# Norms of a two-layer hybrid DiT block: sums of squares kept as a running sum, first weights split before the norm, two modulation units behind it

## The chip, the cores and the metric

The kernel runs on one core of a Trainium2 chip. It is written with a tile framework: the program issues operations in Python order, a list scheduler decides before the run in which order each engine takes its instructions, and every engine then works through its own list in that order. DMAs are issued by SyncE (SP), whose list is in order too. The metric is the device time of one execution in microseconds (us), lower is better. Times of unprofiled runs are given as a median; a profiled execution gives the trace.

## What is computed

A DiT of two layers on 256 context and 256 latent tokens, width 1024, all in float32. In each layer a norm with modulation feeds a mixer of three branches (gated delta net, gated linear attention, differential attention), whose merged output goes through `w_out` into the residual. A second norm with modulation feeds a dense SwiGLU (layer 0) or a mixture of 8 experts of which each token takes 2 (layer 1, latent tokens only). The change concerns the norms and the modulation:

```python
def _rmsnorm(x, g):
    y = x * lax.rsqrt(jnp.mean(jnp.square(x), axis=-1, keepdims=True) + EPS)
    return y * g
def _modulate(x, g, shift, scale):
    return _rmsnorm(x, g) * (1.0 + scale) + shift
...
# shift and scale, and the gates of the residuals, are rows of silu(cond) @ w_mod[l] + b_mod[l]
# (6 x 1024 numbers a layer, one set for context and one for latent tokens)
```

## The kernel before

**Layout.** Everything is held with features on the 128 partitions: `x[0]` and `x[1]` are the context and the latent tokens, 8 k-blocks of 128 features by 256 tokens each. A projection of 128 output features over 512 tokens sums over the 8 k-blocks.

**Matmuls in three parts.** To keep float32 precision, each weight and each activation is split into a high part (a CAST on ScalarE, ACT, in `split`, L269) and a remainder (a subtraction on VectorE, DVE, L270). Each weight tile then takes three matmuls on TensorE (PE): `wh*ah` (L274), `wh*al` (L275), `wl*ah` (L276). Raw weights land in a pool of three buffers of 1 MB (`raw`), the split ones in six tiles (`whl`), enough for three column chunks of 128.

**A norm** (`norm_stats`, L414 on, and `norm_mod`, L434 on). For each half of the tokens: four Squares of two k-blocks each on ACT (L420, 128x512), three adds on DVE (L423), a matmul with ones that sums over partitions (L425), then Ln and Exp on ACT (L410, L411) for the reciprocal root `rs`. Then for each k-block and half: x times `rs` on DVE (L456), the modulation on ACT with scale `A` and shift `B`, which writes the high part `hh` (L457), the same in full precision on DVE (L459), and the remainder `hl` (L461). The norms are named (layer, 1 or 2): (0,1) reads inputs that `norm_only` has normed, (0,2), (1,1) and (1,2) stand behind `mix_out` of layer 0, `ffn` of layer 0 and `mix_out` of layer 1. (1,2) takes the latent half only and feeds the router (L1180).

**Residuals.** `mix_out` (L1121 on) and `ffn` (L1136 on) produce one output block of 128 features after another; behind each, one DVE operation per half adds it to x (`residual`, L1081).

**Modulation units.** `mod_unit` (L340 on) loads 1 MB of `w_mod` and runs 8 matmuls of 32 columns by 256 (L350), which the trace records as 16. A layer has 24 units, in groups of four; `mod_put` (L353 on) closes a group with a copy to SBUF on ACT (L358, tile `modr`), two short matmuls (L361) and two adds (L368). The first units run at the start; the others are spread over the mixers.

**Order of a mixer.** `PLAN` (L27 to L30) is a list of words for each layer; `m1` to `m8` place modulation units, the other words the steps of the branches (`iv` inverts the delta net's chunk matrices, `sc` is its scan, `ga`, `hc`, `gc` and so on are projections). `MOD_AHEAD` (L34 to L36) says which units a mixer takes. Words of a list are only the program order; the scheduler fills PE's waits with matmuls that stand near.

Of the kernel before, what the change touches and what calls it, by code (L numbers as in the profile page):

```python
# [26 lines left out]
PLAN = ("sm ap su m1 pr m1 iv ga1 m1 ga1 m1 ga1 m1 ga1 m1 za m1 sc m8 dec qkB m1 gb1 m1 ha ma vB m1 gla qC m1 kC m2 gc1 m1 "  # L27
        "vC m1 hb dif mb hc m1 mc",
        "sm ap m1 pr ga1 m1 iv ga1 m1 sc za m1 ga1 m1 ga1 m3 gc1 m1 qkB m1 dec vB m1 ha ma gla qC m1 kC m1 vC m1 hb dif mb "
        "hc m2 mc")  # L30
# [4 lines left out]
MOD_AHEAD = ([(0, list(range(u, u + 4))) for u in range(8, 24, 4)] + [(1, list(range(u, u + 4))) for u in range(0, 8, 4)],  # L35
             [(1, list(range(u, u + 4))) for u in range(8, 24, 4)])  # L36
# [162 lines left out]
class Prog:  # L199
# [66 lines left out]

    def split(self, hi, lo, src, n_src=None):

        self.nc.scalar.copy(hi, src)  # L269
        self.nc.vector.tensor_sub(lo, src, hi.bitcast(F32))  # L270
# [8 lines left out]
    def setup(self):  # L279
# [23 lines left out]
        self.pre = {}  # L303
        self.mod = [self.con([128, 48, 2], f"mod{l}") for l in range(2)]
# [78 lines left out]

    def mod_a(self, l, i, k0=0, k1=8):
# [29 lines left out]
    def norm_stats(self, x):  # L414
        nc = self.nc
        p = self.pq()
        sqs = []
        for k in range(0, 8, 2):
            sq = self.sd([2, 256], "sq")
            nc.scalar.activation(sq, x[:, k:k + 2], AF.Square)  # L420
            sqs.append(sq)
            if k:
                nc.vector.tensor_add(sqs[0], sqs[0], sq)  # L423
        for a in range(2):
            nc.tensor.matmul(p[:, :256], self.ones, sqs[0][:, a], start=a == 0, stop=a == 1)  # L425
        return self.rstd(p[:, :256], 256, 1.0 / DM)

    def norm_only(self, xs):

        r = self.norm_stats(xs)  # L430
# [3 lines left out]
    def norm_mod(self, l, i, x, c0, normed=False):  # L434
# [13 lines left out]
        rs = [None if normed else self.norm_stats(xs) for _, _, xs in halves]  # L448
        for k in range(8):
            for (a, m, xs), r in zip(halves, rs):  # L450
                v = slice(a - c0, a - c0 + 256)
                if normed:
                    t = xs[:, k]
                else:
                    t = self.sm([512], "nt")
# [9 lines left out]
    def proj(self, l, u, H, c0=0, c1=512):  # L465

        hh, hl = H
        w = self.pre.pop((l, u), None) or self.load(self.I["win"][l, u], [8, 256])
        for c in range(2):
            wh, wl = self.part(w[:, :, c * 128:(c + 1) * 128])  # L470
# [53 lines left out]
    def small_proj(self, l, H):  # L524
# [3 lines left out]
        wh, wl = self.part(self.load(self.I["wsm"][l], [8, 48]))  # L528
# [592 lines left out]
    def mix_out(self, l, m, x):  # L1121
        c0 = 256 * l
        n = 512 - c0
        mh, ml = self.wide(l, "mh", F32R), self.wide(l, "ml", F32R)
        for k in range(8):
            self.split(mh[k], ml[k], m[k])
        for pr in range(4):
            w = self.load(self.I["wout"][l, pr], [8, 256])
            for c in range(2):
# [4 lines left out]
                self.residual(x, 2 * pr + c, p[:, :n], c0, self.mod[l][:, 16:24])  # L1134

    def ffn(self, x, H):  # L1136
        nc = self.nc
        hh, hl = H
        for half in range(2):
            mh = [self.ch([4, 512], "fh", F32R) for _ in range(3)]  # L1140
            ml = [self.ch([4, 512], "fl", F32R) for _ in range(3)]
            for u in range(11):
                w = self.load(self.I["f13"][half * 11 + u], [8, 256])
                ps = []
                for c in range(2):
                    wh, wl = self.part(w[:, :, c * 128:(c + 1) * 128])
# [8 lines left out]
            for n in range(8):  # L1155
# [6 lines left out]
                self.residual(x, n, p, 0, self.mod[0][:, 40:48])  # L1162

# [117 lines left out]
    def experts(self, base, x):  # L1281
# [118 lines left out]
        for e in range(8):  # L1400
            for fb in range(11):
# [7 lines left out]
                if e == 0 and MOE_AT <= fb < MOE_AT + MOE_PART:  # L1409
                    self.places.append(self.ch([2, 1024], "wp", F32R))  # L1410
                if fb == 2 and e:
# [28 lines left out]
    def mixer(self, l, H):  # L1440
# [5 lines left out]
        for w in PLAN[l].split():  # L1446
            if w == "su":
                self.setup2()
            elif w == "sm":
                self.small_proj(l, H)  # L1450
            elif w == "ap":
# [36 lines left out]
    def run(self):  # L1488
# [4 lines left out]
        for i, _ in enumerate(todo):  # L1493
            if i == 0:
                x = self.load_x()
            if i in PRE:
                u = U_KA + len(self.pre)
                self.pre[0, u] = self.load(self.I["win"][0, u], [8, 256])
# [4 lines left out]
        self.mod_a(0, 1, 6, 8)  # L1503
        for l in range(2):
            H = self.norm_mod(l, 1, x, 0, l == 0)
# [14 lines left out]
            self.mix_out(l, m, x)  # L1520
# [4 lines left out]
            if l == 0:  # L1525
                H = self.norm_mod(l, 2, x, 0)
                self.ffn(x, H)
                for j in range(2):
                    self.dump(f"xf{j}", x[j])
                self.exp_tables()  # L1530
                if self.stop == "l0":
                    break
            else:
                H = self.norm_mod(l, 2, x, 256)
# [4 lines left out]
    def final(self, x):  # L1539
        nc = self.nc  # L1540
        self.exp_tables()
        rs = self.norm_stats(x)
# [30 lines left out]
```

## Time and profile before

| | |
|---|---|
| median of 3 runs | 2596.59 us (2590.91 to 2604.6) |
| profiled execution | 2588.37 us |
| its span, first to last instruction | 2586.3 us |
| mean granted TensorE clock | 0.973 of full speed |
| PE busy | 2444.9 us (95%) |
| DVE busy | 1716.4 us (66%) |
| ACT busy | 1416.6 us (55%) |

Busy times are sums over an engine's instructions. PE is busy nearly all the time, so a microsecond counts where PE waits, or where it runs at half its clock.

### The profile page before, as it was taken

The numbers are of one execution on the slowest core, as the hardware profiler recorded it, in microseconds if no ns is written. First come the engines' busy times: TensorE is split into PE (matmuls) and PEld (weight loads), VectorE is DVE, ScalarE is ACT, GpSimd is POOL, SyncE is SP. The second block draws the span as 40 slices with busy tenths as digits, with TensorE's granted clock in tenths as the row PEclk, the third lists the DMA queues.
The fourth block names the chain that finished last, engine by engine and source line by source line (L and its number), as shares of the span: only waits on it lengthen the run. The fifth ranks groups of instructions, "written<-read, shape, count | busy, mean of one in ns | idle before, by whom it ended". The sixth has DMA issues, their size and how long they took to land.

```text
span 2586.3 us, 35865 instructions
## 1 busy us (share of the span) xinstructions
PE 2444.9 (95%) x13712; PEld 1965.9 (76%) x13712; DVE 1716.4 (66%) x3130; ACT 1416.6 (55%) x2352; POOL 88.2 (3%) x216
## 2 busy tenths in 40 slices
PE   6998999999998999998978999998999999999997
PEld 4786776676676888886867878797878878878876
DVE  5585447756545434336684475767989888988987
ACT  4764343235553332335853433666877777777775
POOL 0000001100120000000000010010000000000000
PEclk8999899999998999999988999998999999999999
DMA  6344332122131223222362232257979899899994
GB/s 266 129 160 157 107 139 99 49 74 74 67 137 66 100 82 120 93 79 85 112 225 77 68 113 81 104 188 288 377 273 355 341 342 356 344 350 353 341 367 182
DMA packets 72707, 473.13 MB, mean 183 GB/s; under 512 B 8208, under 2 KB 10384, under 8 KB 19664
## 3 DMA queue, kind: packets, MB, share of 16 engines
q1 hardware_dynamic: 68208, 464.73, 48.3%
q10 hardware_dynamic: 4320, 6.03, 0.6%
q8 instruction: 110, 1.80, 0.3%
q14 instruction: 69, 0.57, 0.1%
HBM read 463.65 MB, written 7.08 MB: 182 GB/s over the span
## 4 chain that ended last, share of the span: by engine, by line
PE 70%; DVE 6%; ACT 3%; DMA 2%; issue 1%; POOL 0%; ACTq 0%; DVEq 0%; POOLq 0%
PE pm L275 16%; PE pm L274 16%; PE pm L276 16%; PE y L276 3%; PE y L275 3%; PE y L274 3%; PE la L985 1%; DMA raw<-in_win_dram 1%; PE pq L1052 1%; DVE whl L270 1%; PE pm L350 1%; PE tp L1352 1%; PE ob L996 1%; PE ob L998 1%; DVE zq L973 1%
## 5 line engine op out<-in xcount | busy, mean ns | idle before, releaser
L270 DVE TENSOR_TENSOR whl<-raw,whl 128x512 fp32r<-128x512 f32 (+2 forms) x490 | 330.7, 681 | 330.0 <-ACT whl L269 326.7
L274 PE MATMUL pm<-hh,whl 128*128 128x512 f32 (+2 forms) x1264 | 475.6, 378 | 21.3 <-ACT whl L269 7.8
L269 ACT CAST whl<-raw 128x512 fp32r<-128x512 f32 (+2 forms) x490 | 289.6, 600 | 357.1 <-PE pm L276 273.5
L276 PE MATMUL pm<-hh,whl 128*128 128x512 f32 (+2 forms) x1264 | 467.7, 371 | 7.4 <-DVE whl L270 7.4
L275 PE MATMUL pm<-hl,whl 128*128 128x512 f32 (+2 forms) x1264 | 468.3, 371 | 0.0
L270 DVE TENSOR_TENSOR wp<-rawc,wp 128x1024 fp32r<-128x1024 f32 x261 | 313.7, 1222 | 36.6 <-ACT wp L269 30.5
L274 PEld LDWEIGHTS pm<-hh,whl 128*128 128x128 f32 (+1 forms) x1264 | 243.0, 192 | 70.8 <-ACT whl L269 9.2
L269 ACT CAST wp<-rawc 128x1024 fp32r<-128x1024 f32 x261 | 268.1, 1051 | 21.0 <-PE y L276 11.4
L276 PEld LDWEIGHTS pm<-hh,whl 128*128 128x128 f32 (+1 forms) x1264 | 242.3, 192 | 48.9 <-DVE whl L270 8.4
L275 PEld LDWEIGHTS pm<-hl,whl 128*128 128x128 f32 (+1 forms) x1264 | 243.0, 192 | 43.2 <-issue 7.1
L270 DVE TENSOR_TENSOR wlo<-raw,whi 128x1024 fp32r<-128x1024 f32 x176 | 210.0, 1222 | 34.1 <-ACT whi L269 31.7
L275 PE MATMUL pm<-wlo,hg 128*128 128x512 f32 x530 | 212.1, 400 | 1.6 <-DVE wlo L270 1.4
L274 PE MATMUL pm<-whi,hg 128*128 128x512 f32 x530 | 211.2, 399 | 0.0
L276 PE MATMUL pm<-whi,hg 128*128 128x512 f32 x530 | 208.0, 392 | 0.0
L269 ACT CAST whi<-raw 128x1024 fp32r<-128x1024 f32 x176 | 178.9, 1052 | 13.2 <-PE pm L275 11.9
L275 PE MATMUL y<-wp,mt 128*128 128x512 f32 x348 | 135.4, 389 | 0.0
L276 PE MATMUL y<-wp,mt 128*128 128x512 f32 x348 | 135.3, 389 | 0.0
L275 PEld LDWEIGHTS pm<-wlo,hg 128*128 128x128 f32 x530 | 99.8, 188 | 34.6 <-DVE wlo L270 15.8
L274 PE MATMUL y<-wp,mt 128*128 128x512 f32 x348 | 120.1, 389 | 0.2 <-ACT mt L1354 0.2
L274 PEld LDWEIGHTS pm<-whi,hg 128*128 128x128 f32 x530 | 99.9, 189 | 20.8
L276 PEld LDWEIGHTS pm<-whi,hg 128*128 128x128 f32 x530 | 99.8, 188 | 20.2
L270 DVE TENSOR_TENSOR wlo<-rawc,whi 128x1024 fp32r<-128x1024 f32 x91 | 110.9, 1219 | 2.3 <-ACT whi L269 1.5
(394 smaller groups left out, 4528.9 us busy)
## 6 DMA issues: line engine op xcount, KB each, us to landing
rawc<-in_m_dram SPq DMA_DIRECT2D x176, 1024.0 KB, 5.4
raw<-in_m_dram SPq DMA_DIRECT2D x88, 1024.0 KB, 7.0
raw<-in_win_dram SPq DMA_DIRECT2D x64, 1024.0 KB, 5.0
raw<-in_wmod_dram SPq DMA_DIRECT2D x40, 1024.0 KB, 5.0
raw<-in_f_dram SPq DMA_DIRECT2D x22, 1024.0 KB, 4.8
raw<-in_wo_dram SPq DMA_DIRECT2D x24, 512.0 KB, 3.8
raw<-in_f_dram SPq DMA_DIRECT2D x16, 704.0 KB, 4.1
rawc<-in_wmod_dram SPq DMA_DIRECT2D x8, 1024.0 KB, 17.0
```

The lines of the kernel that those rows point to most:

```text
L269: self.nc.scalar.copy(hi, src)
L270: self.nc.vector.tensor_sub(lo, src, hi.bitcast(F32))
L274: mm(p, wh, ah, start=first, stop=False)
L275: mm(p, wh, al, start=False, stop=False)
L276: mm(p, wl, ah, start=False, stop=last)
L350: nc.tensor.matmul(p[j:j + 32, :256], self.cs[:, k, o:o + 32], w[:, k], start=i == 0 and k < 4, stop=i == n - 1 and k >= 4)
L973: nc.vector.tensor_mul(FQ[hp][r, x, a].rearrange("p (n s) -> p n s", s=LEVELS[li]), side(Fj[:, x]), side(q[hp]))
L985: mm(p[:, x % 2, hp], FK[hp][:, x], FQ[hp][:, x], start=True, stop=True)
L996: mm(o[:, hp], vB[:, tt, h * 128:(h + 1) * 128], AT[:, hp, a], start=True, stop=first)
L998: mm(o[:, hp], S[d][r, hp], qe[hp][r], start=False, stop=True)
L1052: mm(p[:, :nk], q[ms, h, cs], k[ms, h, :nk], start=True, stop=True)
L1352: nc.tensor.transpose(tp[:, a], s[:, a * 128:(a + 1) * 128], self.C("ident"))
```

## The change

1. `stats` keeps a running sum of squares. Behind each residual of `mix_out` and `ffn`, two Squares (128x256, one for each half) go to a 512-wide tile and one 512-wide add brings them to `acc`. The last block is not added: `acc` and the last squares `sq` each go through a matmul with ones into the same PSUM bank, followed by one 512-wide Ln and Exp for both halves. ACT's function table for them is loaded ahead of the last block of `ffn` instead of behind it.
2. `norm_mod` does both halves of a k-block together and in two ways. Even blocks: two products on DVE, two modulations on ACT, one 512-wide CAST for `hh`, one 512-wide subtraction for `hl`. Odd blocks: x·A·rs in one DVE operation per half, the shift added on ACT (`hh`), (t + B − hh) in one DVE operation per half (`hl`). `issue_after` makes the scheduler place the products of block k behind the remainder of block k−2.
3. The first weights behind a norm are loaded and split ahead of it: the small projection and the first K unit of the delta net (both layers), the first unit of `ffn`.
4. Two modulation units each stand behind the norms (0,2), (1,1) and (1,2) (`MOD_NORM`); their groups are closed later (`put_late`). The mixers have six units less (22 instead of 24 in layer 0, 12 instead of 16 in layer 1), and `PLAN` loses or moves some of its `m` words. In layer 1 `sc za` now stand behind two more projections `ga1`.

```diff
-PLAN = ("... hb dif mb hc m1 mc", "sm ap m1 pr ga1 m1 iv ga1 m1 sc za m1 ga1 m1 ga1 m3 gc1 m1 ... hc m2 mc")
+PLAN = ("... hb dif mb hc mc", "sm ap m1 pr ga1 m1 iv ga1 m1 ga1 m1 sc za m1 ga1 m2 gc1 m1 ... hc m1 mc")
+MOD_NORM = {(0, 2): (0, [22, 23]), (1, 1): (1, [8, 9]), (1, 2): (1, [22, 23])}
...
+    def stats(self, xs):
+        n = 256 * len(xs)
+        acc = self.sm([512], "acc")
+        seen = []
+        def add(k):
+            sq = acc if not seen else self.sd([512], "sq")
+            for j, x in enumerate(xs):
+                nc.scalar.activation(sq[:, 256 * j:256 * j + 256], x[:, k], AF.Square)
+            seen.append(k)
+            if 1 < len(seen) < 8:
+                nc.vector.tensor_add(acc[:, :n], acc[:, :n], sq[:, :n])
+            if len(seen) < 8:
+                return None
+            p = self.pq()
+            nc.tensor.matmul(p[:, :n], self.ones, acc[:, :n], start=True, stop=False)
+            nc.tensor.matmul(p[:, :n], self.ones, sq[:, :n], start=False, stop=True)
+            return self.rstd(p[:, :n], n, 1.0 / DM)
+        return add
...
-            for (a, m, xs), r in zip(halves, rs):
-                    nc.vector.tensor_mul(t[:, :256], xs[:, k], r[:, :256])
-                nc.scalar.activation(HH[k][:, v], t[:, :256], AF.Identity, bias=B[:, k, m:m + 1],
-                                     scale=A[:, k, m:m + 1])
-                nc.vector.tensor_scalar(t[:, :256], t[:, :256], A[:, k, m:m + 1], B[:, k, m:m + 1],
-                                        op0=OP.mult, op1=OP.add)
-                nc.vector.tensor_sub(HL[k][:, v], t[:, :256], HH[k][:, v].bitcast(F32))
+                if r is not None and k > 1:
+                    es.enter_context(self.tc.issue_after(subs[k - 2].ins))
...
+                    elif r is not None and k % 2 == 0:
+                        nc.vector.tensor_mul(t[:, v], src, r[:, v])
+                    elif r is not None:
+                        nc.vector.scalar_tensor_tensor(t[:, v], src, a, r[:, v], op0=OP.mult, op1=OP.mult)
+            if r is None or k % 2 == 0:
+                for j, (v, a, b, src) in enumerate(vs):
+                    if r is not None or j:
+                        nc.scalar.activation(t[:, v], t[:, v] if r is not None else src, AF.Identity, bias=b, scale=a)
+                nc.scalar.copy(HH[k], t[:, :n])
+                subs.append(nc.vector.tensor_sub(HL[k], t[:, :n], HH[k].bitcast(F32)))
+            else:
+                for v, a, b, src in vs:
+                    nc.scalar.activation(HH[k][:, v], t[:, v], AF.Identity, bias=b)
+                for v, a, b, src in vs:
+                    sub = nc.vector.scalar_tensor_tensor(HL[k][:, v], t[:, v], b, HH[k][:, v].bitcast(F32),
+                                                         op0=OP.add, op1=OP.subtract)
+                subs.append(sub)
+        if (l, i) in MOD_NORM:
+            ml, us = MOD_NORM[l, i]
+            p = self.pq()
+            for j, u in enumerate(us):
+                self.mod_unit(ml, u, j, len(us), p)
+            self.late = ml, us, p
...
+            self.pre[l, "sm"] = self.part(wsm)
+            self.pre[l, U_KA] = self.parts(wk)
+            H = self.norm_mod(l, 1, x, 0, r)
...
+                self.pre["f", 0, 0] = self.parts(self.load(self.I["f13"][0], [8, 256]))
+                H = self.norm_mod(l, 2, x, 0, r)
```

How the lists of the engines differ at three places. The first is PE's list at norm (0,2), from the last matmul of `mix_out` to the first of `ffn` (`pm<-hh,whl`). Before:

```order
L276 MATMUL pm<-mh,whl 128x512
L425 MATMUL pq<-sq,ones 128x256 x4
L274 MATMUL pm<-hh,whl 128x512 x3
L275 MATMUL pm<-hl,whl 128x512
```

and with the change, where `raw,cs` are the modulation units and `cstt,modr` closes the preceding group:

```order
L281 MATMUL pm<-mh,whl 128x512
L444 MATMUL pq<-acc,ones 128x512
L356 MATMUL pq<-raw,cs 32x256 x5
L445 MATMUL pq<-sq,ones 128x512
L356 MATMUL pq<-raw,cs 32x256 x11
L279 MATMUL pm<-hh,whl 128x512 x2
L367 MATMUL pm<-cstt,modr 128x4 x2
```

The two modulation units stand between the sums and the first projection, part of them ahead of the second sum.

The second place is ACT's list at the same norm. Before, with `x_6503` and `x_6504` the two halves of x:

```order
L420 ACTIVATE sq<-x_6503 128x512
L410 ACTIVATE rs<-pq,cb 128x256
L420 ACTIVATE sq<-x_6504 128x512
L411 ACTIVATE rs<-rs,cb 128x256
L420 ACTIVATE sq<-x_6504 128x512 x3
L457 ACTIVATE hh<-nt,mod_84,A_6514 128x256
L410 ACTIVATE rs<-pq,cb 128x256
L411 ACTIVATE rs<-rs,cb 128x256
L457 ACTIVATE hh<-nt,mod_84,A_6514 128x256 x8
```

and with the change:

```order
L437 ACTIVATE sq<-x_6497 128x256
L437 ACTIVATE sq<-x_6498 128x256
L274 CAST whl<-raw 128x512 x2
L422 ACTIVATE rs<-pq,cb 128x512
L423 ACTIVATE rs<-rs,cb 128x512
L364 COPY modr<-pq 128x256
L489 ACTIVATE nt<-nt,mod_84,A_6508 128x256 x2
L494 ACTIVATE hh<-nt,mod_84 128x256
L490 CAST hh<-nt 128x512
L494 ACTIVATE hh<-nt,mod_84 128x256
```

The second half's three Squares behind the first Ln are gone; two CASTs of the second `ffn` unit, the copy `modr`, a second modulation, one of block 1 and a CAST stand in the list up to the first `hh` that a matmul reads.

The third place is PE's list in layer 1's scan of the delta net (`V`, `sp` and `w` are its matmuls). Before, 21 projection matmuls (`hh,whl`, `hl,whl`) and 16 of modulation units (`raw,cs`) stood between its steps, as here:

```order
L767 MATMUL sp<-vk,ktok 128x128 x4
L759 MATMUL V<-vtok,U_10004 128x128 x4
L276 MATMUL pm<-hh,whl 128x256
L274 MATMUL pm<-hh,whl 128x256
L275 MATMUL pm<-hl,whl 128x256
L276 MATMUL pm<-hh,whl 128x256
L274 MATMUL pm<-hh,whl 128x256
L275 MATMUL pm<-hl,whl 128x256
L276 MATMUL pm<-hh,whl 128x256
L274 MATMUL pm<-hh,whl 128x256
L767 MATMUL sp<-vk,ktok 128x128 x4
```

and with the change:

```order
L804 MATMUL V<-vtok,U_10009 128x128 x4
L812 MATMUL sp<-vk,ktok 128x128 x4
L804 MATMUL V<-vtok,U_10010 128x128 x4
L812 MATMUL sp<-vk,ktok 128x128 x4
L791 MATMUL w<-Xs,ktok 128x128 x4
```

No other matmul stands inside this first part of the scan any more; that work has moved ahead of it, into the inversion `iv`.

## Rows read from the trace of the kernel before

**Rows 1.** The page: busy time by engine, and the chain that ended last.

```profile
PE 2444.9 (95%) x13712; PEld 1965.9 (76%) x13712; DVE 1716.4 (66%) x3130; ACT 1416.6 (55%) x2352; POOL 88.2 (3%) x216
...
PE 70%; DVE 6%; ACT 3%; DMA 2%; issue 1%; POOL 0%; ACTq 0%; DVEq 0%; POOLq 0%
```

**Rows 2.** Waits of PE: line, waited for, us in total, times, longest.

```profile
PE pq L425 <- DVE sq L423: 24.6, 8, 4.3
```

**Rows 3.** Timeline of norm (0,2): start, length, engine, line, count, idle before.

```profile
814.81 0.39 PE L276 MATMUL pm<-mh,whl 128*128 128x512 f32 x1
815.24 0.88 DVE L1081 SCALAR_TENSOR_TENSOR x<-pm,mod,x 128x256 f32<-128x256 f32 x2 [1.33 <-PE pm L276]
...
817.37 1.13 PE L425 MATMUL pq<-sq,ones 128*128 128x256 f32 x4 [2.17 <-DVE sq L423]
818.54 0.47 ACT L410 ACTIVATE rs<-pq,cb 128x256 f32<-128x256 f32 x1 [2.10 <-PE pq L425]
...
820.48 2.28 DVE L423 TENSOR_TENSOR sq<-sq 128x512 f32<-128x512 f32 x3
...
822.82 2.08 PE L425 MATMUL pq<-sq,ones 128*128 128x256 f32 x4 [4.32 <-DVE sq L423]
...
825.43 0.51 ACT L411 ACTIVATE rs<-rs,cb 128x256 f32<-128x256 f32 x1
825.98 1.43 DVE L456 TENSOR_TENSOR nt<-x,rs 128x256 f32<-128x256 f32 x4 [2.43 <-ACT rs L411]
826.43 2.08 ACT L457 ACTIVATE hh<-nt,mod,A 128x256 fp32r<-128x256 f32 x4 [0.49 <-DVE nt L456]
...
827.09 1.65 PE L274 MATMUL pm<-hh,whl 128*128 128x512 f32 x3 [2.19 <-ACT hh L457]
```

**Rows 4.** PE's timeline at norm (1,1).

```profile
1189.27 0.39 PE L276 MATMUL pm<-fh,whl 128*128 128x512 f32 x1
...
1201.55 1.51 PE L274 MATMUL pm<-hh,whl 128*48 128x512 f32 x3 [2.20 <-ACT hh L457]
```

**Rows 5.** Copies of `modr` in the whole kernel: durations in ns (min, median, max).

```profile
L358 ACT COPY modr<-pm x14: 350/368/395, 17.7 to 1723.9; 128x256 f32<-128x256 f32 x14
```

**Rows 6.** SP: loads of `ffn` (KB, median us to landing), and its first four's timeline.

```profile
raw<-in_f_dram SPq DMA_DIRECT2D x22, 1024.0 KB, 4.8
...
778.65 32.98 SPq L250 DMA_DIRECT2D raw<-in_f_dram  x4
```

**Rows 7.** Windows: length, busy by engine (count), granted clock, DMA share, GB/s.

```profile
827.10:833.30 6.20, 6.20 (x15) 4.67 (x16) 6.20 (x20) 3.49 (x7) 0.00 (x0) 0.51 0.00 0
...
1201.60:1206.00 4.40, 4.40 (x12) 2.73 (x13) 4.40 (x14) 2.50 (x6) 0.00 (x0) 0.59 0.00 0
...
1305.00:1366.00 61.00, 47.22 (x371) 42.06 (x372) 53.86 (x119) 37.75 (x68) 1.80 (x1) 0.81 0.65 231
...
713.70:717.10 3.40, 3.21 (x6) 1.89 (x7) 0.75 (x1) 1.84 (x5) 0.00 (x0) 0.50 0.99 419
```

**Rows 8.** PE's timeline at a short wait inside layer 0's mixer.

```profile
711.46 1.12 PE L844 MATMUL pm<-sq,ones 128*128 128x512 f32 x2 [2.48 <-ACT sq L842]
```

**Rows 9.** PE's timeline at the start, norm (0,1).

```profile
31.46 1.07 PE L350 MATMUL pm<-rawc,cs 128*32 128x256 f32 x16 [0.98 <-DMA rawc<-in_wmod_dram]
35.73 1.02 PE L361 MATMUL pm<-cstt,modr 128*128 128x4 f32 x4 [3.20 <-ACT modr L358]
39.98 0.66 PE L274 MATMUL pm<-hh,whl 128*48 128x512 f32 x1 [3.24 <-ACT whl L269]
```

**Rows 10.** DVE's timeline: a later group of four products in (0,2), and in (1,2).

```profile
829.96 1.43 DVE L456 TENSOR_TENSOR nt<-x,rs 128x256 f32<-128x256 f32 x4
...
1758.20 1.43 DVE L456 TENSOR_TENSOR nt<-x,rs 128x256 f32<-128x256 f32 x4
...
1762.18 1.22 DVE L270 TENSOR_TENSOR wlo<-rawc,whi 128x1024 fp32r<-128x1024 f32 x1
```

**Rows 11.** DVE by line in layer 1's inversion, 1305 to 1366: busy us, mean ns.

```profile
L270 DVE TENSOR_TENSOR whl<-raw,whl 128x512 fp32r<-128x512 f32 x24 | 16.3, 686 | 2.0 <-ACT whl L269 1.9
```

**Rows 12.** PE's timeline in layer 1's scan.

```profile
1392.37 1.52 PE L746 MATMUL w<-Xs,ktok 128*128 128x128 f32 x8 [1.91 <-DVE Xs L743]
```

More of the change, by code (lines that the diff above doesn't have):

```diff
@@ L34 @@
 MOD_GROUP = 4
-MOD_AHEAD = ([(0, list(range(u, u + 4))) for u in range(8, 24, 4)] + [(1, list(range(u, u + 4))) for u in range(0, 8, 4)],
-             [(1, list(range(u, u + 4))) for u in range(8, 24, 4)])
+MOD_AHEAD = ([(l, list(range(u, v))) for l, u, v in ((0, 8, 12), (0, 12, 16), (0, 16, 20), (0, 20, 22), (1, 0, 4), (1, 4, 8))],
+             [(1, list(range(u, v))) for u, v in ((10, 14), (14, 18), (18, 22))])
+MOD_NORM = {(0, 2): (0, [22, 23]), (1, 1): (1, [8, 9]), (1, 2): (1, [22, 23])}
 def _fm(a, k):
@@ L265, in part, with parts @@
         return H, L
+    def parts(self, w):
+        return [self.part(w[:, :, c * 128:(c + 1) * 128]) for c in range(2)]
     def split(self, hi, lo, src, n_src=None):
@@ L303, in setup @@
         self.pre = {}
+        self.late = None
         self.mod = [self.con([128, 48, 2], f"mod{l}") for l in range(2)]
@@ L382, in mods, with put_late @@
             self.mod_put(*v)
+    def put_late(self):
+        if self.late:
+            self.mod_put(*self.late)
+            self.late = None
     def mod_a(self, l, i, k0=0, k1=8):
@@ L412, in rstd, with norm_mod @@
         return t
-    def norm_stats(self, x):
+    def stats(self, xs):
         nc = self.nc
[L416 to L426, printed above, removed]
+        n = 256 * len(xs)
[15 more added lines that the diff above has]
+        return add
     def norm_only(self, xs):
-        r = self.norm_stats(xs)
+        add = self.stats([xs])
+        for k in range(8):
+            r = add(k)
         for k in range(0, 8, 2):
             self.nc.vector.tensor_mul(xs[:, k:k + 2], xs[:, k:k + 2], r[:, None, :256].to_broadcast([128, 2, 256]))
-    def norm_mod(self, l, i, x, c0, normed=False):
+    def norm_mod(self, l, i, x, c0, r=None):
         nc = self.nc
@@ L527, in small_proj @@
         hh, hl = H
-        wh, wl = self.part(self.load(self.I["wsm"][l], [8, 48]))
+        wh, wl = self.pre.pop((l, "sm"))
         p = self.pm()
@@ L1142, in ffn @@
             for u in range(11):
-                w = self.load(self.I["f13"][half * 11 + u], [8, 256])
+                ws = self.pre.pop(("f", half, u), None)
+                if ws is None:
+                    w = self.load(self.I["f13"][half * 11 + u], [8, 256])
+                if u == 1:
+                    self.put_late()
                 ps = []
                 for c in range(2):
-                    wh, wl = self.part(w[:, :, c * 128:(c + 1) * 128])
+                    wh, wl = ws[c] if ws else self.part(w[:, :, c * 128:(c + 1) * 128])
                     p = self.pm()
@@ L1162, in ffn @@
                 self.residual(x, n, p, 0, self.mod[0][:, 40:48])
+                if half and n == 7:
+                    self.exp_tables()
+                if half:
+                    r = add(n)
+        return r
     def route_cols(self):
@@ L1519, in run @@
                 self.route_cols()
-            self.mix_out(l, m, x)
+            r = self.mix_out(l, m, x)
             for j in range(2):
@@ L1541, in final @@
         self.exp_tables()
-        rs = self.norm_stats(x)
+        add = self.stats([x])
+        for k in range(8):
+            rs = add(k)
         o = self.ch([8, 256], "o")
```

49 lines of the change are left out of this document (30 added, 19 removed).

## The prediction

> **What bounds the kernel now.** I read the page first, then the waits of PE, then the timeline around each norm. PE is busy for 2444.9 of 2586.3 us and makes up 70% of the chain that ended last, where DVE has 6% and ACT 3% [rows 1]. So the time is PE's work plus PE's waits, plus what half clock costs, and ACT or DVE count only where PE waits for them. The waits of PE name the norms: the sums of squares (L425) waited 24.6 us in all, eight times, up to 4.3 us [rows 2].
>
> The timeline of norm (0,2) shows how. The last matmul of `mix_out` ends at 815.20 (814.81 + 0.39), the first of `ffn` starts at 827.09: 11.9 us [rows 3]. In between, the first half's sum is ready at 817.37. The other half's squares stand behind the first Ln (818.54) on ACT, so their three adds run from 820.48 to 822.76 and the second sum starts only at 822.82. Ln and Exp follow (done 825.94), a product at 825.98, `hh` at 826.43, two of which open the projection [rows 3]. At norm (1,1) the same stretch is 1189.66 to 1201.55, 11.9 us again [rows 4]. Behind it PE runs at half clock (1.2 of 2.4 GHz): granted 0.51 over 6.2 us at (0,2) and 0.59 over 4.4 us at (1,1), while it is busy throughout [rows 7].
>
> **The change, step by step**
>
> *Norms (0,2) and (1,1).* I set t = 0 at the end of the last matmul. The residuals are done at 0.9 (0.88 for two, rows as before) [rows 3]. The trace has no 128x256 Square. I bound it by the 128x256 copy, 0.37 [rows 5], and by an `hh` operation of that size, 2.08/4 = 0.52 [rows 3], and take the first, since neither has a per-partition scale: the second square, behind the second residual, ends at 1.4. The Trainium skill (ScalarE: Activation LUTs, What ACT_TABLE_LOAD costs) gives an ACTIVATE with immediate operands a fixed 186 ns beside its elements, which speaks against halving the squares. By its figures 16 halves cost ACT an estimated 0.75 us more a norm, and the last one ends only 0.03 us later than by the copy; ACT has that time, so the sum is the same by either.
>
> PE does the sum of `acc` meanwhile and starts that of the last squares at about 1.7. Four records of 256 columns took 1.13 [rows 3], and I take as much for a 512-wide sum at half the count, so it ends at 2.8. A 512-wide Ln and Exp: the 256-wide ones took 0.47 and 0.51 [rows 3]; at most twice that, 1.96. I take 1.4, because part of each is fixed: Exp is done at 4.2. Then on ACT `modr` (0.37) [rows 5], two modulations (0.52 each), one `hh` of block 1 (0.52) and the CAST (0.37 to 0.74, taken as 0.6): the first projection can start near 6.8. That is 5.1 earlier than 11.9; I take 5.0 for each of the two norms. Bounds: 5.5 if the fixed shares are large, 2 if ACT is held up as in the second rival.
>
> The two modulation units (1.07 each [rows 9]) fall into PE's wait there. They are raw and need no split. PE's own work does not reach the chain, since ACT is late next.
>
> *Clock.* PE still waits some 2.5 us for the first `hh`. Inside layer 0's mixer a wait of 2.48 ahead of the sums at 711.46 [rows 8] was followed by 3.4 us at a granted clock of 0.50 [rows 7], which costs 1.7. At (0,2) now 6.2 us at half clock cost 3.0, at (1,1) 4.4 us cost 1.8 [rows 7]. With one such fall in each place the gain is 1.3 and 0.1: 1.4 in all, between 0 (falls as long as now) and 4.8 (none).
>
> *The products* are pinned: those of block k stand behind the remainder of block k−2. Now DVE takes 3.98 us for two blocks (825.98 to 829.96) [rows 3, 10]. With the change the same two blocks are four products, a 512-wide subtraction and two halves, by the four products' 1.43 [rows 3] and about 2.2 for the remainders 3.7 us: nothing gained or lost while PE stays near it.
>
> *Norm (1,2)* has one half, so the second branch that (0,2) loses was never there. Its first route matmul should come about 0.7 us earlier, but DVE's next blocks go one pair after another: a product, ACT's modulation and CAST, the subtraction, some 0.4 + 0.5 + 0.4 + 0.4 and the hand-overs between, 2.2 to 2.6 per two blocks against (1762.18 − 1758.20)/2 = 2.0 [rows 10]. The two cancel: 0, ± 1. At the end of the kernel the last adds still queue behind residuals: 0.
>
> *Start, (0,1).* PE waits 3.24 us for a cast weight at 39.98, because ACT does sixteen `hh` first, and 3.20 for `modr` at 35.73 [rows 9]. With weights split ahead the first of these goes, the second stays: −2.5, between 0 and −3.2.
>
> *Six modulation units leave the mixers:* 6 × 1.07 = 6.4 us of PE work [rows 9]. Where PE is busy (95% overall [rows 1]) this is won in full; where a unit covered a wait it is not. Layer 1's inversion shows such a place: PE busy 47.22 of 61 us [rows 7], 77%. I take 0.7 of it, −4.5, bounds −6.4 and 0. Two groups more have to be closed, about 0.5 us each at full clock, half of the 1.02 in [rows 9]: +1.0.
>
> *Layer 1's inversion and scan.* `sc za` go behind two more projections. The scan loses its cover of 21 projection matmuls and 16 of modulation, which filled some 4 us (two units 2.1, the rest taken as about 2) between steps like that at 1392.37, where PE waits 1.91 for DVE as it is [rows 12]. They move to the inversion, where PE is idle 13.8 us, but whose chain on DVE takes their splits: 24 of 0.686 us now [rows 11], 8 more by the order, 5.5 us. One gives, the other takes: 0, ± 5.
>
> **Sum.** −2.5 (start) −10.0 (two norms) −1.4 (clock) −4.5 (units) +1.0 (closings) = −17.4 us. The profiled execution took 2588.4, so 2571.0 on that footing. It lies 8.2 below the median of 2596.6; the same difference on the median gives 2579.2.
>
> **Rivals**
>
> *Gain at the norms, given back in the mixers.* The six units come from words behind projections where PE waits for a load or for DVE, so waits open in their place, and the inversion is 5 us longer. For it: PE's 13.8 us of waits there and DVE's 53.86 busy of 61 [rows 7]. Against it: ACT and DVE have slack over the whole. Then −2.5 −10 −1.4 +1 +5 = −8, median 2589, within 0.5% (13 us, about what a measurement of this kernel can tell from no change).
>
> *ACT's list holds the Ln.* Two CASTs of the second `ffn` unit stand ahead of Ln. That unit's load can only be issued when a raw buffer comes free. `ffn`'s first four loads went out over 32.98 us from 778.65, the last near 811.3 [rows 6], and two modulation loads now stand between the first and the second of them, so its load goes out there. Loads of 1 MB land about 5 us after their issue (4.8 [rows 6]), so it lands near 816.3, t = 1.1, ahead of the Ln at 2.8. If it lands 4 us later, Ln waits 2 to 3 us at each norm. The Trainium skill (TensorE: Matmul & The Clock Gate, Architectural detail) calls ACT a strict FIFO, by which every microsecond of that delay would reach Ln; no row of before shows this place. The gain at the norms falls to about 4, the sum to −11, median 2585, within 0.5%.
>
> *Slower.* The pinned products set PE's pace. The price is in each step of DVE's cycle: 3.98 us for two blocks now [rows 3, 10], four such steps in each of two norms. I have 3.7; if ACT's modulation, CAST and second `hh` come one behind the other with DVE waiting at each, a cycle is the products 1.43, ACT's 0.52 × 4 + 0.6, the remainders 2.2, 6.3 in all. Eight steps of 2.3 give 18 back: no change. It decides from about 8 us a step (8 × 4 = 32, +15 net, median 2611), which needs waits that no row shows.
>
> **Chances.** Forecast 0.57, given back in the mixers 0.29, Ln held 0.07, pinned products 0.07. The forecast's own range is 2566 to 2586, by start, clock and inversion (0 to −3.2, 0 to −4.8, ± 5). For eight in ten the second and third case are added up to 2592; the lower end is 2562, with all units won, no fall of the clock and the inversion 5 us shorter (−17.4 − 1.9 − 3.4 − 5 = −27.7, so 2569) less the 7 us by which single runs lie off their median. Faster by more than 0.5% (below 2583.6): most of the first case and little of the second, 0.57. Slower by more than 0.5%: part of the last, 0.06.
>
> **What would show it.** In the profile after: one wait ahead of the first `hh` in each of (0,2) and (1,1), some 7 us from the last matmul to the first; L445's wait near 1 us instead of 4.3; at most one short fall of the clock behind each; the first projection at the start near 37.5; (1,2) unchanged. It would be wrong if Ln starts well behind the second sum, if DVE's products are more than 4 us apart per two blocks, or if PE's waits in 1305 to 1410 have grown by more than 5 us.

## The result and the profile after

The changed kernel takes 2561.07 us (median of 4 runs, 2557.74 to 2562.30), the kernel before 2595.44 beside it (4 runs, 2590.91 to 2604.60): ratio 0.9866, interval 0.984 to 0.9892, 34.4 us less. The forecast was 2579.2 with a range from 2562 to 2592. The direction held; the gain is twice the forecast, and the time lies 0.9 us below the range.

The page of the changed kernel, as in [rows 1]:

```profile
PE 2436.4 (95%) x13712; PEld 1961.6 (77%) x13712; DVE 1708.4 (67%) x3082; ACT 1424.9 (56%) x2394; POOL 86.5 (3%) x216
...
PE 73%; DVE 6%; ACT 3%; issue 1%; DMA 1%; POOL 0%; ACTq 0%; DVEq 0%; POOLq 0%
```

PE is 8.5 us less busy with the same number of instructions (13712). The span is 26.5 us shorter, so PE's idle time is 18 us less.

The waits of PE, as in [rows 2] (line, waited for, us in total, times, longest):

```profile
PE pq L444 <- DVE acc L440: 11.9, 4, 4.3
...
PE v L744 <- ACT W L722: 7.3, 1, 7.3
```

The sums' wait falls from 24.6 to 11.9 us; what is left stands at the start and at the final norm. New is one wait of 7.3 us in layer 1's inversion.

Norm (0,2) in the timeline of all engines, as in [rows 3]:

```profile
808.30 0.39 PE L281 MATMUL pm<-mh,whl 128*128 128x512 f32 x1
...
808.53 1.02 PE L444 MATMUL pq<-acc,ones 128*128 128x512 f32 x2
808.73 0.88 DVE L1126 SCALAR_TENSOR_TENSOR x<-pm,mod,x 128x256 f32<-128x256 f32 x2 [3.36 <-PE pm L281]
809.25 0.81 ACT L437 ACTIVATE sq<-x 128x256 f32<-128x256 f32 x2 [4.63 <-DVE x L1126]
...
809.97 1.12 ACT L274 CAST whl<-raw 128x512 fp32r<-128x512 f32 x2
...
810.46 1.12 PE L445 MATMUL pq<-sq,ones 128*128 128x512 f32 x2
...
811.62 0.69 ACT L422 ACTIVATE rs<-pq,cb 128x512 f32<-128x512 f32 x1 [0.54 <-PE pq L445]
...
813.07 0.37 ACT L364 COPY modr<-pq 128x256 f32<-128x256 f32 x1
813.10 0.76 DVE L483 TENSOR_TENSOR nt<-x,rs 128x256 f32<-128x256 f32 x2 [1.21 <-ACT rs L423]
...
814.96 0.60 ACT L490 CAST hh<-nt 128x512 fp32r<-128x512 f32 x1
...
815.61 0.73 PE L279 MATMUL pm<-hh,whl 128*128 128x512 f32 x2 [2.60 <-DVE hl L496]
...
816.60 0.75 DVE L483 TENSOR_TENSOR nt<-x,rs 128x256 f32<-128x256 f32 x2
```

From the last matmul's end (808.69) to the first of `ffn` (815.61) it takes 6.9 us instead of 11.9. Ln starts at 811.62, at once behind the sum; the two CASTs ahead of it had run at 809.97. DVE's products come every 3.50 us for two blocks (813.10, 816.60).

PE at norm (1,1), as in [rows 4]: the units (L356) fill the time between the sums and the wait.

```profile
1176.62 0.39 PE L281 MATMUL pm<-fh,whl 128*128 128x512 f32 x1
1176.85 1.02 PE L444 MATMUL pq<-acc,ones 128*128 128x512 f32 x2
1177.80 1.05 PE L356 MATMUL pq<-raw,cs 128*32 128x256 f32 x10
1178.78 1.13 PE L445 MATMUL pq<-sq,ones 128*128 128x512 f32 x2
1179.84 1.50 PE L356 MATMUL pq<-raw,cs 128*32 128x256 f32 x22
1183.93 0.44 PE L279 MATMUL pm<-hh,whl 128*48 128x512 f32 x1 [2.60 <-ACT hh L490]
```

The start, as in [rows 9]: the wait for a cast weight is gone, the one for `modr` is longer.

```profile
37.55 1.01 PE L367 MATMUL pm<-cstt,modr 128*128 128x4 f32 x4 [4.61 <-ACT modr L364]
38.42 0.64 PE L279 MATMUL pm<-hh,whl 128*48 128x512 f32 x1
```

**Where the time went.** I cut the span at PE's marks: first and last projection of a stage, the last `o` of a scan, the last `ob` of the gated linear attention and, in layer 1, the first `v`, the matmul with which the inversion begins to join its blocks. Times are read from the timelines. The microseconds at half clock are summed from the trace's own entries of the granted clock, which are finer than the two digits of the rows. The kernel before has two profiles (the second is an experiment below).

| stage | before | before, again | changed | half clock: before | again | changed |
|---|---|---|---|---|---|---|
| start to first projection | 40.0 | 39.4 | 38.4 | 12.4 | 10.0 | 9.3 |
| layer 0: to the scan's end | 254.5 | 254.0 | 253.8 | 8.1 | 7.0 | 7.8 |
| layer 0: to the end of gated linear attention | 270.5 | 276.9 | 260.1 | 13.7 | 27.3 | 7.7 |
| layer 0: to the end of `mix_out` | 250.2 | 250.3 | 256.4 | 3.4 | 3.4 | 19.6 |
| norm (0,2) | 11.9 | 11.9 | 6.9 | 7.6 | 7.8 | 0.0 |
| `ffn` | 362.6 | 362.5 | 361.4 | 6.1 | 5.9 | 3.4 |
| norm (1,1) | 11.9 | 11.9 | 6.9 | 6.6 | 6.7 | 0.0 |
| layer 1: to the inversion's first `v` | 164.7 | 167.6 | 163.3 | 27.6 | 30.9 | 14.2 |
| layer 1: to the scan's end | 64.5 | 64.8 | 67.8 | 6.8 | 6.8 | 23.4 |
| layer 1: to the end of `mix_out` | 319.3 | 317.6 | 307.7 | 17.1 | 10.2 | 3.4 |
| norm (1,2) to the end | 836.3 | 836.7 | 837.1 | 29.4 | 31.5 | 28.8 |
| span | 2586.3 | 2593.5 | 2559.8 | 138.6 | 147.5 | 117.5 |

Start, norms and `ffn` give 12.7 us against the first profile of before, 12.0 against the second. The two mixers (the six stretches of the two layers) give 14.6 and 22.1. Nothing else moves by more than 1 us. From the first profile to the changed kernel, 21 us at half clock go, 17 of them at the two norms and in `ffn`. In the mixers they are 77 us before, 86 in its second profile and 76 with the change: there half clock has moved from some stretches to others.

### The profile page after: what moved, and what is told of

Same layout as the page of the kernel before. It is cut to its first block, busy times and chain, and to the rows that moved or that the text cites. A ratio compares the mean times of both kernels' runs of the same rounds, so it can differ in the third digit from the quotient of the medians.

```text
span 2559.8 us, 35870 instructions
## 1 busy us (share of the span) xinstructions
PE 2436.4 (95%) x13712; PEld 1961.6 (77%) x13712; DVE 1708.4 (67%) x3082; ACT 1424.9 (56%) x2394; POOL 86.5 (3%) x216
## 4 chain that ended last, share of the span: by engine, by line
PE 73%; DVE 6%; ACT 3%; issue 1%; DMA 1%; POOL 0%; ACTq 0%; DVEq 0%; POOLq 0%
PE pm L280 17%; PE pm L279 17%; PE pm L281 17%; PE y L281 3%; PE y L280 3%; PE y L279 3%; PE la L1030 2%; PE pq L1097 1%; DMA raw<-in_win_dram 1%; PE tp L1411 1%; PE ob L1041 1%; PE ob L1043 1%; PE pm L889 1%; DVE ATb L1032 1%; PE oc L1114 1%
## 5 line engine op out<-in xcount | busy, mean ns | idle before, releaser
L279 PE MATMUL pm<-hh,whl 128*128 128x512 f32 (+2 forms) x1264 | 473.6, 376 | 12.9 <-DVE zs L852 5.2
L279 PEld LDWEIGHTS pm<-hh,whl 128*128 128x128 f32 (+1 forms) x1264 | 240.5, 190 | 64.8 <-issue 9.3
L274 ACT CAST wp<-rawc 128x1024 fp32r<-128x1024 f32 x261 | 267.7, 1049 | 21.2 <-PE y L281 11.1
L274 ACT CAST whi<-raw 128x1024 fp32r<-128x1024 f32 x176 | 179.0, 1052 | 14.5 <-PE pm L280 11.9
```

The source lines that it names most:

```text
L279: mm(p, wh, ah, start=first, stop=False)
```

## Experiments

Times are medians; "above the changed kernel" compares with its second set of runs, 2560.5, beside which the kernel before took 2595.13.

**Norms alone, units alone.** The first kernel is the changed one with plan and lists of before and no units behind norms; the second is the kernel before with the changed plan, lists and units behind its old norms.

```diff
 # first
-PLAN, MOD_AHEAD: changed;  MOD_NORM = {(0, 2): ..., (1, 1): ..., (1, 2): ...}
+PLAN, MOD_AHEAD: of before;  MOD_NORM = {}
 # second, in the kernel before
+PLAN, MOD_AHEAD, MOD_NORM, put_late: changed
```

> The changed kernel with the plan and the lists of modulation units of before and no units behind the norms: norms and early splits alone. Theory (the norms and the start give what they show at their own places, some 11 to 12 us, and the mixers' 15 us come from the six units and the new order of words): 9 to 14 us under before. Rival (the mixers gain because the norms leave clock, buffers or loads in a better state, whatever the plan): 22 us or more under before.

> The kernel before with the changed plan, the changed lists of units and two units behind each of the three norms, but the old norms and no early splits. Theory: the mixers' 15 us come with the plan alone, so 12 to 18 us under before, the waits of the old norms holding the six units without cost. Rival (the units only pay because the new norms leave a place for them): 0 to 6 us under before.

Norms alone took 2588.96 (12 runs, 2577.68 to 2595.53), ratio 0.9977 (0.9961 to 0.9992): 6 us under before, less than the theory's 9 to 14, and far from the rival's 22. At the norms themselves the gain is all there: 6.6 us from last to first matmul instead of 11.9. But layer 0's gated linear attention takes 278.0 us in its profile, at a mean clock of 0.94:

```profile
291.20:569.20 278.00, 260.56 (x1406) 196.03 (x1405) 161.18 (x485) 95.39 (x200) 25.96 (x112) 0.94 0.25 88
```

Units alone took 2581.33, ratio 0.995 (0.9931 to 0.9969): 13.7 us under before, as the theory had it. Behind the old norms the units have a price: they stand behind the second sum and delay the first projection.

```profile
821.77 2.08 PE L433 MATMUL pq<-sq,ones 128*128 128x256 f32 x4 [4.32 <-DVE sq L431]
823.77 3.01 PE L352 MATMUL pq<-raw,cs 128*32 128x256 f32 x32
826.72 0.73 PE L275 MATMUL pm<-hh,whl 128*128 128x512 f32 x2
```

13.1 us there instead of 11.9; the new norms take 6.9 with units and 6.6 without. The two parts sum to 20 us, the whole is 34, so they are not independent. Why is open; the profile of the first has 102 us at half clock in the mixers, where the kernel before has 77 and 86.

**One layer's units back.** In the changed kernel, one layer gets its units and its plan of before back.

```diff
 # layer 0
-"... gc1 vC m1 hb dif mb hc mc"        MOD_NORM = {(0, 2): ..., (1, 1): ..., (1, 2): ...}
+"... gc1 m1 vC m1 hb dif mb hc m1 mc"  MOD_NORM = {(1, 1): ..., (1, 2): ...}
 # layer 1
-"... iv ga1 m1 ga1 m1 sc za m1 ga1 m2 gc1 ... qC kC vC m1 ... hc m1 mc"
+"... iv ga1 m1 sc za m1 ga1 m1 ga1 m3 gc1 ... qC m1 kC m1 vC m1 ... hc m2 mc"  MOD_NORM = {(0, 2): ...}
```

> The changed kernel with layer 0's two units and its plan of before back in the mixer, none behind norm (0,2). Two units are 2.1 us of PE. If the gain is PE's work alone: 1.5 to 3 us above the changed kernel. If the plan of layer 0 decides whether the clock falls in the gated linear attention: 8 to 14 us above it, with a lower mean clock and a spread of 10 us.

> The changed kernel with layer 1's four units and its plan of before back in the mixer, none behind norms (1,1) and (1,2). If PE's work alone counts: 4 to 5 us above the changed kernel. If the plan of layer 1 brings waits and a low clock of its own: 10 to 15 us above it, most of it between the scan and the end of the merge, where four units and their closings stood.

2573.38 (2569.97 to 2578.92) and 2573.72 (2570.27 to 2583.99): 12.9 and 13.2 us above the changed kernel, each as its second theory had it. Together that is 26 us; norms alone, which has the units of both layers back, lies 28.5 above. Two units, 2.1 us of PE by the expectation, cost 13 us in layer 0, and the profile has them in the stage that was slow above. The rows of that stage and the next for that kernel, then the same two and layer 1's three for the changed one:

```profile
291.30:569.30 278.00, 260.68 (x1405) 195.78 (x1405) 161.05 (x485) 95.32 (x200) 25.98 (x112) 0.94 0.25 89
569.30:819.30 250.00, 239.58 (x1123) 181.46 (x1123) 131.60 (x268) 123.55 (x254) 26.02 (x16) 0.99 0.26 93
```

```profile
292.20:552.30 260.10, 244.36 (x1370) 185.99 (x1369) 158.79 (x481) 92.84 (x195) 25.97 (x112) 0.99 0.25 87
552.30:808.70 256.40, 245.72 (x1123) 186.87 (x1124) 134.20 (x270) 125.28 (x257) 25.66 (x16) 0.96 0.26 90
...
1183.90:1347.20 163.30, 148.82 (x997) 124.97 (x998) 130.99 (x292) 118.73 (x232) 2.92 (x3) 0.96 0.45 162
1347.20:1415.00 67.80, 55.53 (x743) 50.22 (x744) 23.18 (x50) 15.39 (x30) 0.00 (x0) 0.83 0.05 17
1415.00:1722.70 307.70, 293.19 (x2054) 249.99 (x2053) 198.80 (x492) 157.10 (x359) 28.82 (x78) 0.99 0.31 109
```

In the first of these stretches the mean clock tells the time at half clock, 2 × (1 − 0.94) × 278 = 33 us against 5; the trace's entries give 34 against 8. PE is busy 16.3 us longer there, for 35 records more. But the stretch ends at the last `ob`, and the two orders do not put the same matmuls ahead of it: among the 35 are 16 of a unit and 4 of a closing, and the rest are projections of 256 columns that the changed kernel does behind that mark. In the next stretch the changed kernel is the slower one, 256.4 us against 250.0, with 20 us at half clock against 3. So the whole mixer of layer 0 has to be compared: 781.4 us against 770.3, 11.1 more. The units' matmuls are 3.3 of it (31.5 us of PE against 28.1) and PE's idle time 1.3. Half clock is 45 us against 35, 5 us at half speed. The rest is not told apart.

With layer 1's units back the same three stretches of layer 1 read:

```profile
1181.80:1347.20 165.40, 147.92 (x960) 122.88 (x960) 127.42 (x284) 116.05 (x224) 2.92 (x3) 0.91 0.41 145
1347.20:1415.50 68.30, 59.22 (x803) 51.78 (x803) 26.23 (x55) 16.28 (x34) 0.00 (x0) 0.90 0.16 55
1415.50:1734.70 319.20, 303.48 (x2096) 258.53 (x2095) 199.28 (x495) 159.79 (x363) 29.70 (x78) 0.98 0.33 114
```

552.9 us against 538.8. PE is busy 13.1 us more and idle 1.0 more. The units' matmuls take 23.3 us of PE here instead of 15.7, so four units are 7.6 and not 4 × 1.07 = 4.3. Half clock, from the trace's entries, is 53 us against 41; at half speed that is 5.8 us. With the idle time these sum to 14.4, where 14.1 were measured. Closings do not count: this mixer has four in both kernels, since the changed one closes the group of norm (1,1) in it.

**The two units elsewhere in layer 0.** In the layer-0 kernel above, the two words move.

```diff
 # ahead of the gated linear attention
-"... za m1 sc m8 dec ... gc1 m1 vC m1 hb dif mb hc m1 mc"
+"... za m1 sc m10 dec ... gc1 vC m1 hb dif mb hc mc"
 # at the end
+"... za m1 sc m8 dec ... gc1 vC m1 hb dif mb hc m2 mc"
```

> The changed kernel with layer 0's two units back in the mixer, none behind norm (0,2), but placed with the eight behind the scan, so that the gated linear attention keeps the changed kernel's order on PE (600 projection matmuls from its first to its last step, where the kernel before has 563). Theory (the order in that stage decides on the clock, not the number of units): 1 to 4 us above the changed kernel, half clock in the stage under 20 us. Rival (two more units in layer 0 cost 13 us wherever they stand): 10 to 14 us above.

> The same two units placed behind the last head projection of layer 0, where the gated linear attention then has 568 projection matmuls from its first to its last step, near the order of before. Theory (the order decides): 8 to 13 us above the changed kernel, half clock in the stage over 25 us. Rival (place of the units within the stage decides, and here they stand behind it): 1 to 4 us above.

Ahead: 2562.67 (2557.53 to 2564.22), ratio 0.9872 (0.9847 to 0.9896). At the end: 2567.29 (2564.44 to 2570.47), ratio 0.9900 (0.9877 to 0.9924). 2.2 and 6.8 us above the changed kernel. Beside these two the kernel before took 2592.61 and not 2595.13, so both differences may be some 2.5 us larger. So two more units in layer 0 cost 2 to 5 us if they stand well, little more than their work; 13 us is a matter of where they stand. Ahead, they run in one piece each: up to the scan's end the units' matmuls take 21.05 us of PE instead of 18.91, 1.07 for each of the two. The stage, units ahead and units at the end:

```profile
292.10:555.60 263.50, 249.33 (x1383) 190.85 (x1382) 159.38 (x481) 93.51 (x196) 25.85 (x112) 0.97 0.25 89
```

```profile
292.60:561.40 268.80, 250.12 (x1394) 190.03 (x1394) 160.52 (x485) 95.42 (x200) 25.96 (x112) 0.98 0.24 88
```

The first expectation is met, with 16 us at half clock by its row. The second is not: the time lies between its two theories, and the clock is 0.98, 11 us at half clock, where I had over 25. Over layer 0's mixer that kernel has 21 us at half clock, less than the changed one's 35, and still takes 771.7 us against 770.3. So the order of the list alone does not settle the clock, and the clock alone does not settle the time.

**One kernel, several executions.** Kernel before, changed kernel, and a variant of the changed kernel with layer 1's `sc za` back ahead of two `ga1`, were each profiled again.

```diff
-"... iv ga1 m1 ga1 m1 sc za m1 ga1 m2 gc1 ..."
+"... iv ga1 m1 sc za m1 ga1 m1 ga1 m2 gc1 ..."
```

> The changed kernel with one thing back: in layer 1 the scan and the z projection stand ahead of the second and third gate projection, as before, with the same number of units. If the order in layer 1 gives part of the gain: 3 to 8 us above the changed kernel. If only the number of units in the mixers matters: within 2 us of it.

> The kernel before, profiled a second time. Its first profile took 2588.4 us, its timed runs have a median of 2595. If the difference is falls of the clock in layer 0's gated linear attention: 2593 to 2600 us with two or three falls of 6.8 us there that the first profile does not have, and the other stages within 1.5 us of it. If it is spread evenly: no stage differs by more than 2 us.

> The changed kernel once more, beside the others on one chip: 2556 to 2564 us. If its spread is again under 6 us where the kernel before has 12, the falls of the clock that spread the kernel before are rare in it.

> The changed kernel, profiled a third time. If the clock in layer 0's gated linear attention follows the kernel: half clock from the end of the scan to the end of that stage is again under 9 us and the time 2556 to 2564 us. If it falls by chance in each execution: one of the two further profiles has 15 us or more there.

> The changed kernel, profiled a fourth time. As the third: under 9 us at half clock in layer 0's gated linear attention if that follows the kernel, 15 us or more in one of the two if it is chance.

> The kernel with the scan ahead of two gate projections in layer 1, profiled again. It ran 7 us above the changed kernel, but its layer 1 took as long and its layer 0, the same instructions, 5 to 7 us longer with 20.5 us at half clock. If that follows the kernel: again 17 to 24 us at half clock in that stage and 2564 to 2571 us. If it is chance: one of the two has under 9 us and 2561 or less.

> The same kernel, profiled a third time. As the second: 17 to 24 us at half clock in that stage of layer 0 if it follows the kernel, under 9 us in one of the two if it is chance.

The kernel before took 2595.63 in its second profile, with 276.9 us in that stage instead of 270.5 and 167.6 in layer 1's inversion instead of 164.7; every other stage is within 1.7 us of the first (table above). That is its first theory but for the inversion. The stage, in its first and its second profile:

```profile
294.50:565.00 270.50, 252.36 (x1406) 189.72 (x1405) 161.07 (x485) 95.22 (x200) 25.98 (x112) 0.97 0.26 91
```

```profile
293.40:570.30 276.90, 256.81 (x1405) 194.38 (x1405) 161.24 (x485) 95.33 (x200) 25.98 (x112) 0.95 0.25 89
```

The same instructions take 6.4 us longer, with 27 us at half clock instead of 14. Over 17 runs the kernel before spreads from 2588.11 to 2599.90, and the fastest five have mean clocks of 0.974 to 0.976, the slowest five 0.968 to 0.971.

The changed kernel took 2560.50 (2558.47 to 2564.45), then 2560.35 and 2557.20. In its four profiles the stage takes 260.1, 259.7, 267.0 and 259.9 us. The third one:

```profile
292.30:559.30 267.00, 248.35 (x1370) 190.49 (x1369) 159.04 (x480) 92.86 (x195) 25.75 (x112) 0.96 0.24 85
```

The variant took 2567.63 (2564.75 to 2570.15), then 2563.61 and 2561.78; its stage takes 266.9, 260.1 and 260.1 us at 0.96, 0.98 and 0.98. So the falls in this stage come by execution. With the changed order the stage takes about 260 or about 267 us; with the order of before it took 270.5, 276.9, 278.0 and 278.0 in four profiles. An estimated 3.4 us of that are the unit, the closing and the projections on the other side of the mark (1.07 + 0.5 + 15 × 0.12, where 0.12 is the distance of two such projections in the timeline). Up to the end of `mix_out` the two orders take 513.7 to 519.4 us (four profiles of the changed kernel) and 520.7 to 529.6.

Six of the variant's eight executions lie above all eleven of the changed kernel, so it is slower: by 7 us on the medians, by 4 in the later profiles, beside which the changed kernel took 2560.35 and 2557.20. That its order in layer 1 is the cause is not shown. Layer 1's mixer takes 542.1, 544.6 and 538.8 us in its three profiles and 537.4 to 541.7 in the changed kernel's four, and the first of the three has its excess in layer 0.

**Three smaller parts.** Without the early splits, without the six units (their shares of the modulation left at zero), and without the pinning of products:

```diff
-            self.pre[l, "sm"] = self.part(wsm); self.pre[l, U_KA] = self.parts(wk)
-                self.pre["f", 0, 0] = self.parts(self.load(...))
 # second
-MOD_NORM = {(0, 2): (0, [22, 23]), (1, 1): (1, [8, 9]), (1, 2): (1, [22, 23])}
+MOD_NORM = {}
 # third
-                    es.enter_context(self.tc.issue_after(subs[k - 2].ins))
```

> The changed kernel without the early splits: the first weights of each consumer are loaded and split where the consumer stands. Theory (they help at the start only): 1 to 3 us above the changed kernel, with the first projection of the start at 39 to 41 us. Rival (at the norms the splits come late and hold the first matmul): 2 to 4 us more at each of the two large norms, so 6 to 10 us above.

> The changed kernel without the six units behind the norms (their shares of the modulation are left at zero, which the output shows); plan and lists stay. If the norms host them at no cost: 0 to 2 us under the changed kernel. If they delay the first projection there or take loads: 3 to 6 us under it.

> The changed kernel without the rule that places the products of a block behind the remainder two blocks back. If the pinning does nothing for the end: within 1.5 us of the changed kernel. If unpinned products crowd out remainders that PE waits for: 2 to 6 us above it, with waits of PE for the remainder behind norms (0,2) and (1,1).

Without early splits 2565.43 (2561.14 to 2567.11), 4.9 above, between its two theories: the first projection starts at 40.2 instead of 38.4, the norms take 6.9 us as in the changed kernel, and the stage of layer 0 takes 266.1 in this profile. So 1.8 of it is the splits' own, at the start; the rest is not told apart from the stage's chance. Without the six units 2562.40 (2561.62 to 2566.95): not under the changed kernel, where both theories had it, so the new norms host them for nothing that can be measured. Without pinning 2561.98 (2559.17 to 2566.57), 1.5 above, with 2592.61 for the kernel before beside it: no difference that these runs can tell, and both norms take 6.9 us in its profile too.

## Why the prediction was right and wrong

**Norms (0,2) and (1,1): right.** Forecast 6.8 us to the first matmul and −5.0 each; measured 6.9, 5.0 less at each. The steps agree: second square done at 1.4 (809.25 + 0.81 less 808.69), second sum 2.9 against 2.8, Exp 4.4 (813.07) against 4.2. The row of the second sum (L445) has no idle time ahead of it, where the other half's sum had 4.3. Two squares of 128x256 took 0.81, 0.41 each and not the copy's 0.37; the Trainium skill's formula (ScalarE: Activation LUTs, What ACT_TABLE_LOAD costs) gives 0.40, and here it was the nearer. By the busy time of their lines, 21.3 us for 56 of these squares against 19.0 for 32 of 128x512, sixteen halves instead of eight cost ACT 1.3 us more a norm, not the 0.75 of the estimate; ACT had the time.

**Clock behind the norms: right at (0,2), too little at (1,1).** Forecast 1.3 and 0.1 us, one short fall left in each place. Behind (0,2) one is left: PE now loses (1 − 0.72) × 6.2 = 1.7 us instead of 3.0, a gain of 1.3, and `ffn` is 1.2 us shorter. At (1,1) the profile shows none, its 4.4 us are at full clock now, a gain of 1.8:

```profile
815.60:821.80 6.20, 6.19 (x22) 5.02 (x23) 5.72 (x15) 4.04 (x9) 0.00 (x0) 0.72 0.52 219
1183.90:1188.30 4.40, 4.37 (x21) 3.28 (x22) 4.39 (x12) 3.31 (x7) 0.00 (x0) 1.00 0.75 318
```

**Products and (1,2): right.** 3.50 us for two blocks against 3.7, and no effect of the pinning. (1,2) to the end is 0.8 us longer than in the first profile of before, forecast 0; 0.5 of it is the closing that has moved there.

**Start: over by 0.9.** −1.6 instead of −2.5, since the wait for `modr` grew from 3.20 to 4.61.

**The rivals.** Ln was not held: the CASTs began 1.6 us ahead of it and ended before the sum did, so no run here tested what a late load would do to ACT's list. The pinned products did not set the pace. And the mixers did not give the gain back but added to it.

**"Six modulation units leave the mixers" is the step that failed: its term was far too small.** I had −4.5 for the units, bound −6.4, and 0 ± 5 for layer 1's inversion and scan. Measured in the mixers are −14.6 on the same profile, −22.1 against the second one. (The +1.0 for two closings was right, but it falls in `ffn` and behind norm (1,2), 0.5 us each; the mixers have ten closings in both kernels.)

I took 1.07 us for a unit, from a row at the start in which its 16 matmuls stand in one piece, and 0.7 of that because some units covered waits. In the mixers many units run in pieces. Of the two in layer 1's scan before, the first is broken into three, which take 1.9 us at full clock:

```profile
1384.26 0.62 PE L350 MATMUL pm<-raw,cs 128*32 128x256 f32 x2
1386.12 0.64 PE L350 MATMUL pm<-raw,cs 128*32 128x256 f32 x8
1388.45 0.63 PE L350 MATMUL pm<-raw,cs 128*32 128x256 f32 x6
```

Over the six stretches, the units' matmuls alone (L350 before, L356 with the change) keep PE busy for:

```profile
sum 1323.60, PE 54.70 PEld 18.88; mean PE 9.12 PEld 3.15
```

```profile
sum 1309.10, PE 43.82 PEld 15.92; mean PE 7.30 PEld 2.65
```

That is 10.9 us for six units, 1.8 each, out of 13.4 by which PE is less busy there. Records of neighbours overlap these in part; counted from each start to the next one, the units give 10.4. PE's idle time in the two mixers (length less busy time, over the six stretches of the table) is 75.6 us before and 74.5 after. It has moved within layer 1, from 7.2 to 12.3 us behind the first `v` and from 18.7 to 14.5 ahead of it, but on balance no wait opened where a unit left, so the units' time was won in full. What is left of the 14.6, 2.5 us of other matmuls, no row tells apart.

I also costed the mixers at a constant clock. In the sum that did no harm, since the two profiles have 77 and 76 us at half clock there; I have no evidence that the 14.6 us come from the clock. But where the units and their words stand does move it, and the experiments show a price. With the units of layer 0 or layer 1 back, that layer's mixer has 10 or 12 us more at half clock, which is 5 and 6 of the 11 and 14 us that it takes longer. Two units placed ahead of the gated linear attention cost only 2 to 5 us. How the rest divides between pieces and clock is worked out from one profile each and not from an experiment that changes one of them alone.

Layer 1's inversion and scan, forecast 0 ± 5, took 229.2 before and 231.1 after, while PE ran 997 records ahead of the scan instead of 960 and 743 in it instead of 803; the shortening shows in what follows, 319.3 to 307.7. PE's idle time in the two went from 25.9 to 26.7 us, so the sign of being wrong, 5 us more of waits, did not come.

**The second failed step is the carrying over.** The sum was made against a profile of 2588.4 and moved to the median by adding 8.2. That profile was one of the shortest executions of the kernel, whose 17 runs lie between 2588.1 and 2599.9; the second profile took 2595.6, with 6.4 of the 7.2 us in one stage. The changed kernel spreads less, its eleven executions lie between 2557.2 and 2564.5, so its profile and its median agree, and the 8.2 was part of the gain. On the profiled footing the change gave 26.7, on the medians 34.4. The forecast's own range also does not follow from its terms, which give 2570 to 2588 and not 2566 to 2586; the result lies below either.

Open is what in layer 0's stage makes the clock fall in some executions and not in others, why the new norms and the new plan give 20 us apart and 34 together, and what makes up the 7 us of units at the end.

## What to carry to other kernels

Work that is hosted in a wait is worth its own time where it left, and that time is read from the place that it leaves: the six units that left the mixers had taken 1.8 us of TensorE each, where one in a single piece takes 1.07. Look also at the clock, of the stretch that it left and of the next one, before a fall is called gone: here half clock moved from stretch to stretch, and its sum over the mixers stayed. Where the runs of a kernel spread by more than its profile's rows explain, find the stage that differs between two executions before a sum from one profile is moved to the median.

## What was not expected of the hardware

The same instructions of one stage took 260 or 267 us in different executions of the changed kernel, at mean granted clocks of 0.98 or 0.99 and of 0.96. In the order of before that stage took 270.5 to 278.0 at 0.97 to 0.94. Between the first and the third profile of the changed kernel, 13 us more at half clock lengthened the stage by 6.9 us, of which 2.9 were waits and 4.0 busy time of PE. And the 16 matmuls of a modulation unit, 1.07 us in one piece, took 1.9 us in three pieces at full clock.
